# Two-block layer with a product-key expert layer: top-k and gathers interleaved, one-hot keys moved to ScalarE, weight placing split in two halves

## The chip, the cores and the metric

The kernel runs on one core of a Trainium2 chip. The metric is the device time of one execution in microseconds (us); the median of three runs is compared. A core has five engines that each run their own instruction stream in program order: PE (TensorE, matmuls), DVE (VectorE), ACT (ScalarE), POOL (GpSimd) and SP (SyncE, which here only starts transfers). They meet through semaphores.

## The reference, cut to what matters

256 tokens of width 2048 pass through two transformer blocks in fp32. The change touches only the expert layer near the end of the second block:

```python
def peer(xn, w_pq, sub_k1, sub_k2, expert_u, expert_v):
    q = (xn @ w_pq).reshape(B, S, 8, 2, 128)          # 8 heads, 2 halves
    s1, s2 = scores of q[..., 0, :] and q[..., 1, :]   # 128 sub-keys each
    v1, i1 = lax.top_k(s1, 16); v2, i2 = lax.top_k(s2, 16)
    cand = (v1[..., :, None] + v2[..., None, :]).reshape(B, S, 8, 256)
    vs, ci = lax.top_k(cand, 16)
    e1 = take(i1, ci // 16); e2 = take(i2, ci % 16)
    eidx = e1 * 128 + e2                               # one of 16384 experts
    gates = softmax(vs)
    act = gelu(einsum('tkd,td->tk', expert_u[eidx], x))     # k: 8 heads x 16 = 128
    return einsum('tk,tkd->td', act * gates, expert_v[eidx])
```

(Two lines are put in words.) So each token picks 128 experts; for each it needs a row of `expert_u` (2048 numbers, 8 KB) and a row of `expert_v`.

## The kernel before

Tokens lie on the 128 partitions, in two halves of 128 tokens (tt = 0, 1). The expert layer runs in these stages, with the span's microseconds of the profiled execution:

- **Top-k (1524 to 1666).** While PE ends the query projection (`project1`), `topk` (L1587) works through the 8 heads one after the other, two generators taking every second head. DVE finds the top 16 of each key half (MAX, MAX_INDEX, MATCH_REPLACE), POOL adds the 16 x 16 candidates (L1600), DVE finds their top 16, POOL splits each winner's position into row and column with seven small operations (L1605 to L1611), DVE compares these with 0..15 (four one-hot compares of 256, L1617), POOL multiplies by the key numbers (four products, L1618), DVE sums (four reduces, L1623) and POOL forms the expert index (six operations, L1625 to L1627). `slots_` then makes e1T, e2T (the two key numbers of each slot, transposed).
- **u rows (1666 to 2312).** `u_rows` gathers for each of the 256 slots (128 for each half of the tokens) one row per token: an indirect DMA of 128 x 8 KB = 1 MB that POOL issues (L1661), into one of 10 buffers in the first half and 4 in the second. DVE multiplies and sums it with the token (L1695, "sum" from here on), which frees the buffer. The first 10 gathers are issued in one block as soon as head 0 has its index; sums start when all heads have theirs. After the 128th sum PE turns the other tokens into PSUM (`turn`, L1657), and `weights` makes the slot weights w of the half that is done.
- **Weights into the table.** The left half of `expert_v`'s columns is not gathered. `spots(tt)` builds the dense table G (16384 experts x 256 tokens, in 8 slabs G0 to G7 of 16 key numbers e1 each): for a group of 8 tokens it makes a one-hot Q of e2 and a one-hot P of e1, scales P by w, and PE multiplies them (L1752, 8 products of 128 x 128); ACT copies the result into the 8 slabs (`put`, L1729). There are 16 groups in each half. `spots(0)` runs beside the second half of the u rows: Q on ACT (Abs and Relu, L1740/41), P on DVE (L1742), scaling on ACT (L1747). `spots(1)` runs in the gap (2312 to 2393) between the last u sum and the main loop: Q and P on DVE (L1737, L1742), scaling on POOL (L1744).
- **Main loop (from 2393).** 128 chunks k of `w_vd` (512 KB each, streamed by SP through 4 buffers) x 8 matmuls (L1848) use G. Beside it `v_rows` gathers the right half of `expert_v`'s columns, 0.5 MB for each of 256 slots (L1661, 8 buffers), and DVE adds them up (L1788, L1790), two rows for each chunk. After the last row PE turns the result (L1769), and the chunks that remain follow. `L1845` lets POOL wait for each chunk's data ("beat"), which paces the gathers. The output projection comes after.

What sets the order: every stage is a Python generator in one of five lanes. `lanes.step()` runs once for each weight chunk, lane 4 (`u_rows`, `v_rows`) a second time in the main loop, and `beside()` steps lanes 2, 3 and 4 (two heads' `topk` and `u_rows`) after every second matmul of `project1`. The build therefore fixes each engine's order; what runs late holds up everything behind it on its engine.

An fp32 matmul leaves two records in the trace, so 8 matmuls are x16.

Of the kernel before, what the change touches and what calls it, by code (L numbers as in the profile page):

```python
# [15 lines left out]
T = 256  # L16
# [209 lines left out]
def program(tc, A, out, stage=99, dbg=None):  # L226
# [1304 lines left out]
    subk, qring, eg = cK(8, 2, 128), cK(4, T), cK(2, 3, 128)  # L1531
# [54 lines left out]
    def topk(first):  # L1586
# [4 lines left out]
        xf = cT(2, 16)  # L1591
        for h in range(first, 8, 2):
# [42 lines left out]
    def slots_():
# [3 lines left out]
        G.tensor_copy(gate_, eg[:, :, 2])  # L1639
# [33 lines left out]
    def u_rows():  # L1673
        seat = [n % 10 if n < 128 else n % 4 for n in range(256)]
        m, busy = 0, {}
        for n in range(256):
            tt, s = divmod(n, 128)
            if n == 0:
                turn(0)
                while not all(flags.get(("idx", h)) for h in range(8)):  # L1680
                    while m < 10 and flags.get(("idx", m // 16)):
                        gather(row[seat[m]], A["w_u"], m)
                        busy[seat[m]] = m
                        m += 1
                    yield
# [217 lines left out]
```

## Time and profile before

| | before |
|---|---|
| median of 3 runs | 3009.86 us (3007.61 to 3015.71) |
| profiled execution, its own time | 3011.99 us |
| its span on the core | 3010.2 us |
| PE busy | 2274.8 us (76%) |
| DVE busy | 2035.2 us (68%) |
| ACT busy | 985.2 us (33%) |
| POOL busy | 936.6 us (31%) |
| first u sum starts | 1665.79 us |
| last u sum ends | 2311.55 us |
| main loop starts | 2393.40 us |
| last of the v rows turned, remaining chunks start | 2858.05 us |

An engine's share is an average over stages with different limits: PE is at work nearly all of the time in the first 1500 us and nearly idle during the u rows. What a stage is worth is read from the stage itself: which wait ends last in it, and whether the DMA engines are full.

### The profile page before, as it was taken

To read this page: it belongs to the slowest core of one execution; us is meant where nothing else is said; L and a number is where in the kernel's file an instruction comes from. 1 tells how busy PE (TensorE), PEld (TensorE's weight loads), DVE (VectorE), ACT (ScalarE), POOL (GpSimd) and SP (SyncE) were. 2 spreads that over 40 slices of the span, in tenths; PEclk is the share of its full clock that TensorE was granted. 3 is DMA by queue.
4 is the path that set the end of the run, shared out by engine and by line. 5 is a ranking of instruction groups with operands and counts; after the bars stand their busy time and mean duration, and the time that the engine had idled before them with its cause. 6 is when DMAs were issued, how large, how long until landed. Compare 5 with 4: busy or idle time off the path is not lost.

```text
span 3010.2 us, 38442 instructions
## 1 busy us (share of the span) xinstructions
PE 2274.8 (76%) x14379; PEld 2059.6 (68%) x14379; DVE 2035.2 (68%) x2663; ACT 985.2 (33%) x1952; POOL 936.6 (31%) x1281
## 2 busy tenths in 40 slices
PE   8999999999999999999978000022111699999899
PEld 8877898888889999998967000022110687877689
DVE  5555566555556565656447999989897966666646
ACT  4355554444444454444411000055530200000043
POOL 3202225111110000330145433333334755555420
PEclk9999999999999999999989555555555899999999
DMA  6443455555655555544564899999998599999945
GB/s 221 153 127 120 132 162 186 189 189 187 196 189 189 183 182 183 163 133 128 196 239 125 334 422 422 422 383 385 385 397 342 176 409 410 409 409 409 365 151 165
DMA packets 174668, 765.04 MB, mean 254 GB/s; under 512 B 19584, under 2 KB 22048, under 8 KB 141200
## 3 DMA queue, kind: packets, MB, share of 16 engines
q1 hardware_dynamic: 99216, 353.83, 35.6%
q0 software_dynamic: 75264, 408.75, 34.0%
q8 instruction: 113, 1.85, 0.3%
q14 instruction: 75, 0.61, 0.1%
HBM read 757.77 MB, written 4.21 MB: 253 GB/s over the span
## 4 chain that ended last, share of the span: by engine, by line
PE 51%; DMA 21%; issue 9%; DVE 9%; POOL 8%; ACT 1%; SPq 0%; POOLq 0%; DVEq 0%; ACTq 0%
DMA rows<-w_vs,idx 13%; PE acc L411 11%; DMA rows<-w_u,idx 7%; PE acc L386 6%; PE acc L388 6%; PE acc L387 6%; PE acc L412 6%; POOL rows L1661 5%; DVE rows L1695 3%; PE acc L485 3%; PE acc L483 3%; PE acc L484 3%; PE acc L1848 1%; PE acc L456 1%; DVE sacc L1790 1%
## 5 line engine op out<-in xcount | busy, mean ns | idle before, releaser
L350 DVE TENSOR_TENSOR wlo<-raw,whi 128x1024 fp32r<-128x1024 f32 (+1 forms) x501 | 613.8, 1233 | 418.4 <-ACT whi L349 411.5
L349 ACT CAST whi<-raw 128x1024 fp32r<-128x1024 f32 (+1 forms) x501 | 519.9, 1042 | 385.2 <-PE acc L387 131.2
L1695 DVE SCALAR_TENSOR_TENSOR rows<-rows,yt 128x2048 f32<-128x2048 f32 x256 | 579.1, 2286 | 48.4 <-DMA rows<-w_u,idx 45.7
L1848 PE MATMUL acc<-G,raw 128*128 128x256 f32 x2048 | 459.8, 385 | 25.7 <-DMA raw<-w_vd 23.7
L1848 PEld LDWEIGHTS acc<-G,raw 128*128 128x128 f32 x2048 | 390.5, 193 | 94.4 <-DMA raw<-w_vd 39.3
L1790 DVE SCALAR_TENSOR_TENSOR sacc<-rows,sm,sacc 128x1024 f32<-128x1024 f32 x254 | 327.3, 1289 | 155.1 <-DMA rows<-w_vs,idx 152.8
L1661 POOL DMA_INDIRECT rows<-w_u,idx x256 | 251.1, 981 | 385.2 <-DVE rows L1695 260.3
L1661 POOL DMA_INDIRECT rows<-w_vs,idx x256 | 255.2, 997 | 201.6 <-DVE sacc L1790 153.3
L1752 PE MATMUL sp<-P,Q 128*128 128x128 f32 x512 | 104.7, 388 | 220.6 <-ACT P L1747 187.2
L1752 PEld LDWEIGHTS sp<-P,Q 128*128 128x128 f32 x512 | 96.9, 292 | 228.4 <-ACT P L1747 191.6
L411 PE MATMUL acc<-xl,whi 128*128 128x512 f32 x704 | 248.3, 392 | 0.0
L411 PE MATMUL acc<-xh,whi 128*128 128x512 f32 x704 | 248.2, 391 | 0.0
L1657 PE MATMUL yt<-keep,xg 128*128 128x128 f32 x32 | 5.4, 342 | 304.1 <-DVE rows L1695 303.5
L564 POOL TENSOR_TENSOR acc_sq<-acc_sq,sq 128x256 f32<-128x256 f32 x63 | 56.9, 903 | 504.5 <-ACT sq L563 502.7
L1657 PEld LDWEIGHTS yt<-keep,xg 128*128 128x128 f32 x32 | 5.0, 182 | 304.7 <-DVE rows L1695 303.9
L485 PE MATMUL acc<-ring,wlo 128*128 128x256 f32 x704 | 199.3, 283 | 0.1
L483 PE MATMUL acc<-ring,whi 128*128 128x256 f32 x704 | 199.3, 283 | 0.1
L484 PE MATMUL acc<-ring,whi 128*128 128x256 f32 x704 | 199.2, 283 | 0.0
L412 PE MATMUL acc<-xh,wlo 128*128 128x256 f32 x704 | 197.2, 280 | 0.0
L412 PE MATMUL acc<-xl,wlo 128*128 128x256 f32 x704 | 197.1, 280 | 0.0
L1191 POOL TENSOR_TENSOR hT<-cF 128x256 f32<-128x256 f32 x44 | 70.9, 1611 | 372.6 <-ACT whi L349 342.7
L386 PE MATMUL acc<-xl,whi 128*128 128x256 f32 x520 | 153.2, 295 | 0.0
(476 smaller groups left out, 5343.7 us busy)
## 6 DMA issues: line engine op xcount, KB each, us to landing
raw<-w_gu SPq DMA_DIRECT2D x176, 512.0 KB, 4.2
raw<-w_vd SPq DMA_DIRECT2D x128, 512.0 KB, 6.8
raw<-w_down SPq DMA_DIRECT2D x88, 512.0 KB, 4.4
raw<-w_out SPq DMA_DIRECT2D x32, 512.0 KB, 3.6
raw<-w_pq SPq DMA_DIRECT2D x32, 512.0 KB, 3.6
raw<-w_pg SPq DMA_DIRECT2D x32, 512.0 KB, 4.0
raw<-w_b SPq DMA_DIRECT2D x24, 512.0 KB, 3.6
raw<-w_lat SPq DMA_DIRECT2D x18, 512.0 KB, 3.6
```

Of the source, the lines that this page charges most:

```text
L349: S.copy(hi[j][:, a:b], raw[j][:, a:b])
L350: V.tensor_sub(lo[j][:, a:b], raw[j][:, a:b], hi[j][:, a:b].bitcast(F32))
L386: PE.matmul(ps, wh, xh, start=start, stop=False, **k)
L411: PE.matmul(ps, wh, xh.both(k), start=k == 0, stop=False, skip_group_check=True)
L412: PE.matmul(ps[:, :T], wl, xh[:, k], start=False, stop=k == kb - 1, skip_group_check=True)
L483: PE.matmul(o, wh, ah, start=(k == 0 and j % 2 == 0), stop=False, skip_group_check=True)
L484: PE.matmul(o, wh, al, start=False, stop=False, skip_group_check=True)
L485: PE.matmul(o, wl, ah, start=False, stop=(k == nk - 1), skip_group_check=True)
L1661: G.indirect_dma_start(dst, None, src, bass.IndirectOffsetOnAxis(ap=idx[:, tt, s:s + 1], axis=0))
L1695: V.scalar_tensor_tensor(r, r, 1.0, accT, op0=OP.mult, op1=OP.mult, accum_out=wv[:, tt, s:s + 1])
L1790: V.scalar_tensor_tensor(sacc, r, w, sacc, op0=OP.mult, op1=OP.add)
L1848: PE.matmul(o, w, gs_[k // 16][:, k % 16], start=(k == 0 and j % 2 == 0), stop=k == 127, skip_group_check=True)
```

## The change

It has five parts.

1. **Top-k.** The four compares become one of 1024, ahead of the four POOL products; the four reduces become one; POOL's six index operations become three over both halves of the tokens. The exponential is emitted one step later, and there is one step more between products and reduce. The key numbers now lie in `ek`, and `slots_` copies them (4 POOL copies) before the transposes.
2. **u rows.** One gather per step instead of ten in a block, and the sums start when 4 of the 8 heads have their indices.
3. **`spots(0)`.** P is made on ACT like Q: 16 more ACT operations for each group, no DVE operation.
4. **`spots(1)`.** Two halves of 64 key numbers. Half 0 (G0 to G3) is placed before the main loop, with P of 64 columns and 4 copies for each group. Half 1 (G4 to G7) is placed inside the loop's first 62 chunks: Q and scaling on ACT, narrow P on DVE, one group every 4 chunks.
5. **`v_rows`.** The first 8 gathers are issued two per step, and never more than two per step after that.

The diff, cut to its core:

```diff
@@ topk
+            io = iota[:, 0:16][:, None, :].to_broadcast([128, 64, 16])
+            yield
+            sel = oh.rearrange("p t s a b -> p (t s a) b")
+            V.tensor_tensor(sel, flat(c1)[:, :, None].to_broadcast([128, 64, 16]), io, op=OP.is_equal)
+            for tt, s in both:
+                G.tensor_mul(oh[:, tt, s], oh[:, tt, s], iif[:, tt, s][:, None, :].to_broadcast([128, 16, 16]))
             for tt in range(2):
-                S.activation(eg[:, tt, 2, hs], vs[:, tt], AF.Exp, bias=gs[:, tt, 0:1], accum_out=gs[:, tt, 1:2])
-            io = iota[:, 0:16][:, None, :].to_broadcast([128, 16, 16])
-            yield
-            for tt, s in both:
-                V.tensor_tensor(oh[:, tt, s], c1[:, tt, s][:, :, None].to_broadcast([128, 16, 16]), io, op=OP.is_equal)
-                G.tensor_mul(oh[:, tt, s], oh[:, tt, s], iif[:, tt, s][:, None, :].to_broadcast([128, 16, 16]))
-            yield
-            yield
+                S.activation(eg[:, tt, hs], vs[:, tt], AF.Exp, bias=gs[:, tt, 0:1], accum_out=gs[:, tt, 1:2])
+            yield
+            yield
+            yield
+            V.tensor_reduce(flat(ek[:, h]), sel, axis=AX.X, op=OP.add)
             V.reciprocal(gs[:, :, 2], gs[:, :, 1])
-            for tt, s in both:
-                V.tensor_reduce(eg[:, tt, s, hs], oh[:, tt, s], axis=AX.X, op=OP.add)
...
@@ u_rows
+        def more(most):
+            while most and ask[0] < 256 and seat[ask[0]] not in busy and flags.get(("idx", ask[0] % 128 // 16)):
+                m = ask[0]
+                gather(row[seat[m]], A["w_u"], m)
+                busy[seat[m]] = m
+                ask[0] += 1
+                most -= 1
...
+        while heads() < 4:
+            more(1)
+            yield
         for n in range(256):
             tt, s = divmod(n, 128)
-            if n == 0:
-                turn(0)
-                while not all(flags.get(("idx", h)) for h in range(8)):
-                    while m < 10 and flags.get(("idx", m // 16)):
-                        gather(row[seat[m]], A["w_u"], m)
...
+            for _ in range(2 if heads() < 8 else 0):
+                more(1)
                 yield
+            more(2)
+            while n >= ask[0]:
+                yield
+                more(1)
...
@@ spots
+        if not tt:
+            for n in range(16):
...
+                lit(Q, i, t0)
                 for k in range(8):
-                    S.activation(Q[:, k], iota, AF.Abs, bias=gs_["n"][:, t0 + k:t0 + k + 1])
-                    S.activation(Q[:, k], Q[:, k], AF.Relu, scale=-1.0, bias=one)
-            V.tensor_tensor(P, io, e1T[:, ts][:, :, None].to_broadcast(wide), op=OP.is_equal)
...
+                    S.activation(P[:, k], iota, AF.Abs, bias=gs_["m"][:, t0 + k:t0 + k + 1])
+                    S.activation(P[:, k], P[:, k], AF.Relu, scale=-1.0, bias=one)
...
+        else:
+            for half in range(2):
+                lo, p = half * 64, None
+                for n in range(16):
...
+                    if half:
+                        lit(Q, i, t0)
+                    else:
+                        V.tensor_tensor(Q, io, e2T[:, ts][:, :, None].to_broadcast(wide), op=OP.is_equal)
+                    Pn = P[:, :, 0:64]
+                    V.tensor_tensor(Pn, iota[:, lo:lo + 64][:, None, :].to_broadcast(narrow),
+                                    e1T[:, ts][:, :, None].to_broadcast(narrow), op=OP.is_equal)
+                    if half:
+                        for k in range(8):
+                            S.activation(P[:, k, 0:64], P[:, k, 0:64], AF.Identity, scale=wT[:, t0 + k:t0 + k + 1])
+                        for _ in range(2):
+                            yield
+                    else:
+                        G.tensor_mul(Pn, Pn, wT[:, ts][:, :, None].to_broadcast(narrow))
...
+                    for k in range(8):
+                        PE.matmul(p[:, at + k * 64:at + k * 64 + 64], Q[:, k], P[:, k, 0:64], start=True, stop=True)
...
+                    if half and n % 2:
+                        put(range(4, 8), t0 - 8, p, 16)
+                    elif not half:
+                        put(range(4), t0, p[:, 0:512], 8)
+                    yield
+                flags[("g", 1, half)] = True
@@ v_rows
-            while m < 256 and m % 8 not in busy:
...
+            for _ in range(4 if n == 0 else 1):
+                for _ in range(2):
+                    if m < 256 and m % 8 not in busy:
...
+                if n == 0:
+                    yield
@@ main loop
-    until(("g", 1))
+    until(("g", 1, 0))
...
+        if k == 62:
+            until(("g", 1, 1))
```

`lit` is the pair of ACT loops that made Q before, as a function.

**DVE, around the fifth head (head 4).** Before, one head from the index search to the next head's first MAX (L1617 compares, L1621 reciprocal, L1623 reduces):

```order
L1583 MAX_INDEX cT<-cT 128x8 x2
L1617 TENSOR_TENSOR cT<-cT,keep 128x256 x4
L1621 RECIPROCAL cT<-cT 128x2
L1623 TENSOR_REDUCE cK<-cT 128x16 x4
L1572 MAX cT<-sc 128x8 x4
```

After, the end of head 4 (L1703 is the u sum, L1616 the merged compare, L1624 the merged reduce):

```order
L1580 MAX cT<-cT 128x8 x2
L1703 SCALAR_TENSOR_TENSOR rows_15108,sm<-rows_15108,yt 128x2048
L1583 MAX_INDEX cT<-cT 128x8 x2
L1616 TENSOR_TENSOR cT<-cT,keep 128x1024
L1703 SCALAR_TENSOR_TENSOR rows_15108,sm<-rows_15108,yt 128x2048
L1624 TENSOR_REDUCE cK<-cT 128x64
L1625 RECIPROCAL cT<-cT 128x2
L1703 SCALAR_TENSOR_TENSOR rows_15109,sm<-rows_15109,yt 128x2048 x2
L1703 SCALAR_TENSOR_TENSOR rows_15110,sm<-rows_15110,yt 128x2048
L1572 MAX cT<-sc 128x8 x4
```

Between the reduce of head 3 and that of head 7 there now stand 25 sums on DVE (6, 7, 7 and 5 for the four heads); before there was none. One of them stands between every compare and its reduce.

**POOL, behind the first head's index.** Before (L1661 is the gather, L1632 the gate, L1598 to L1600 the next head's candidates):

```order
L1627 CAST idx<-cT 128x16
L1661 DMA rows_15106<-w_u,idx 128x2048 x2
L1661 DMA rows_15107<-w_u,idx 128x2048 x2
L1661 DMA rows_15108<-w_u,idx 128x2048 x2
L1661 DMA rows_15109<-w_u,idx 128x2048 x2
L1661 DMA rows_15110<-w_u,idx 128x2048 x2
L1632 TENSOR_SCALAR cK<-cK,cT 128x16 x2
L1598 CAST cT<-cT 128x64
L1600 TENSOR_TENSOR cT<-cT 128x256 x2
```

After (L1663 is the gather, L1601 the candidates):

```order
L1628 CAST idx<-cT 128x2x16
L1663 DMA rows_15106<-w_u,idx 128x2048
L1633 TENSOR_SCALAR cK<-cK,cT 128x16 x2
L1599 CAST cT<-cT 128x64
L1601 TENSOR_TENSOR cT<-cT 128x256 x2
L1663 DMA rows_15106<-w_u,idx 128x2048
L1663 DMA rows_15107<-w_u,idx 128x2048 x2
L1663 DMA rows_15108<-w_u,idx 128x2048 x2
L1606 CAST cT<-cT 128x32
```

The ten gathers no longer stand ahead of the candidates of the next head in one block; 10 stand ahead of head 4's index, and 34 ahead of head 7's.

**PE, from the second half's groups on.** Before (L1752 a group's products, L1848 the loop's matmuls, L1769 the turning of the v sums, L386 the output projection; x128 is 16 chunks):

```order
L1752 MATMUL sp<-P,Q 128x128 x128
L1848 MATMUL acc<-G_16381,raw 128x256 x128
...
L1848 MATMUL acc<-G_16388,raw 128x256 x56
L1769 MATMUL tok<-keep,rows_15106 128x128 x8
L1848 MATMUL acc<-G_16388,raw 128x256 x72
L386 MATMUL acc<-pl,whi 128x256
```

After (L1794 the groups, L1900 the loop, L1815 the turning):

```order
L1794 MATMUL sp<-P,Q 128x64 x128
L1900 MATMUL acc<-G_16313,raw 128x256 x8
L1794 MATMUL tok<-P,Q 128x64 x8
L1900 MATMUL acc<-G_16313,raw 128x256 x32
L1794 MATMUL tok<-P,Q 128x64 x8
...
L1900 MATMUL acc<-G_16320,raw 128x256 x64
L1815 MATMUL tok<-keep,rows_15106 128x128 x8
L1900 MATMUL acc<-G_16320,raw 128x256 x64
L386 MATMUL acc<-pl,whi 128x256
```

All 128 products of half 0 stand ahead of the loop; the 16 groups of half 1 stand inside it, the first after one chunk, then one every four. Behind the last turning stand 8 chunks instead of 9. On DVE 12 v sums stand ahead of the loop instead of 16.

## Rows read from the trace of the kernel before

**Rows 1.** Windows: stretch, length, each engine's busy time (instructions), PEclk, DMA share, GB/s
```profile
1524.00:1666.00 142.00, 97.24 (x460) 83.94 (x459) 100.83 (x457) 18.69 (x78) 76.51 (x180) 0.87 0.50 171
...
2312.00:2393.00 81.00, 45.23 (x257) 41.66 (x257) 69.03 (x52) 23.25 (x130) 67.01 (x44) 0.73 0.47 151
2393.00:2845.00 452.00, 427.41 (x1911) 362.94 (x1912) 299.70 (x235) 2.07 (x6) 243.24 (x350) 0.98 1.03 408
```

**Rows 2.** Timeline, DVE, top-k: start, duration, line, operation, count [idle before <-releaser]
```profile
1560.62 1.00 DVE L1572 MAX8 cT<-cT 128x8 f32<-128x256 f32 x2 [12.88 <-POOL cT L1600]
...
1602.49 0.86 DVE L1572 MAX8 cT<-sc 128x8 f32<-128x128 f32 x4
...
1608.16 1.00 DVE L1572 MAX8 cT<-cT 128x8 f32<-128x256 f32 x2 [0.91 <-POOL cT L1600]
...
1613.58 0.42 DVE L1617 TENSOR_TENSOR cT<-cT,keep 128x256 f32<-128x256 f32 x1 [1.39 <-POOL cT L1608]
1614.52 2.15 DVE L1617 TENSOR_TENSOR cT<-cT,keep 128x256 f32<-128x256 f32 x3 [0.52 <-POOL cT L1610]
...
1665.79 2.28 DVE L1695 SCALAR_TENSOR_TENSOR rows<-rows,yt 128x2048 f32<-128x2048 f32 x1
...
1667.99 2.28 DVE L1695 SCALAR_TENSOR_TENSOR rows<-rows,yt 128x2048 f32<-128x2048 f32 x1
```

**Rows 3.** Timeline, POOL, first and last of ten gathers behind head 0's index
```profile
1546.87 1.08 POOL L1661 DMA_INDIRECT rows<-w_u,idx  x1 [0.18 <-issue]
...
1558.21 0.94 POOL L1661 DMA_INDIRECT rows<-w_u,idx  x1 [0.30 <-issue]
```

**Rows 4.** Groups by line, top-k stretch: count | busy, mean ns | idle before
```profile
L1618 POOL TENSOR_TENSOR cT<-cT 128x256 f32<-128x256 f32 x32 | 26.4, 853 | 0.0
```

**Rows 5.** Timeline, DVE, second half of the u rows
```profile
1973.65 2.29 DVE L1695 SCALAR_TENSOR_TENSOR rows<-rows,yt 128x2048 f32<-128x2048 f32 x1 [2.41 <-PE yt L1657]
...
1998.29 2.29 DVE L1695 SCALAR_TENSOR_TENSOR rows<-rows,yt 128x2048 f32<-128x2048 f32 x1 [0.19 <-DMA rows<-w_u,idx]
...
2000.78 2.29 DVE L1695 SCALAR_TENSOR_TENSOR rows<-rows,yt 128x2048 f32<-128x2048 f32 x1 [0.19 <-DMA rows<-w_u,idx]
```

**Rows 6.** Groups by line, second half of the u rows: the one-hot P
```profile
L1742 DVE TENSOR_TENSOR P<-keep,sq 128x1024 f32<-128x1024 f32 x16 | 19.5, 1220 | 0.0
```

**Rows 7.** Timeline, ACT, first group beside the u rows: pairs, scaling, copies
```profile
1973.92 0.40 ACT L1740 ACTIVATE Q<-keep,ne 128x128 f32<-128x128 f32 x1
...
1979.75 2.43 ACT L1747 ACTIVATE P<-P,acc_sq 128x128 f32<-128x128 f32 x8
1983.84 1.45 ACT L1729 COPY G<-sp 128x128 f32<-128x128 f32 x8 [1.66 <-PE sp L1752]
```

**Rows 8.** Timeline, DVE, gap before the main loop: first group, two later ones
```profile
2311.55 1.22 DVE L1737 TENSOR_TENSOR Q<-keep,sq 128x1024 f32<-128x1024 f32 x1
...
2349.51 2.01 DVE L1737 TENSOR_TENSOR Q<-keep,sq 128x1024 f32<-128x1024 f32 x1
...
2353.77 2.01 DVE L1737 TENSOR_TENSOR Q<-keep,sq 128x1024 f32<-128x1024 f32 x1
```

**Rows 9.** Timeline, POOL, same gap: first scaling, slowest of the first gathers
```profile
2314.31 1.90 POOL L1744 TENSOR_TENSOR P<-P,acc_sq 128x1024 f32<-128x1024 f32 x1 [1.23 <-DVE P L1742]
...
2325.39 1.91 POOL L1661 DMA_INDIRECT rows<-w_vs,idx  x1 [0.30 <-DVE sacc L1790]
```

**Rows 10.** Timeline, PE: a group, the loop's start, and its end
```profile
2363.27 2.05 PE L1752 MATMUL sp<-P,Q 128*128 128x128 f32 x16 [0.62 <-POOL P L1744]
...
2393.40 133.10 PE L1848 MATMUL acc<-G,raw 128*128 128x256 f32 x608 [1.54 <-ACT G L1729]
2526.95 3.72 PE L1848 MATMUL acc<-G,raw 128*128 128x256 f32 x16 [0.44 <-DMA raw<-w_vd]
...
2856.29 1.97 PE L1769 MATMUL tok<-keep,rows 128*128 128x128 f32 x8 [10.75 <-ACT rows L1797]
2858.05 32.56 PE L1848 MATMUL acc<-G,raw 128*128 128x256 f32 x144
```

More of the change, by code (lines that the diff above doesn't have):

```diff
@@ L1591, in topk @@
         xf = cT(2, 16)
+        flat = lambda v: v.rearrange("p t s n -> p (t s n)")
         for h in range(first, 8, 2):
@@ L1638, in slots_ @@
             yield
[L1639 removed]
+        G.tensor_copy(gate_, eg)
         for tt in range(2):
@@ L1674, in u_rows @@
         seat = [n % 10 if n < 128 else n % 4 for n in range(256)]
-        m, busy = 0, {}
+        done, busy, ask = [0], {}, [0]
+        def more(most):
[5 more added lines that the diff above has]
+                most -= 1
+        heads = lambda: sum(bool(flags.get(("idx", h))) for h in range(8))
+        turn(0)
+        while heads() < 4:
+            more(1)
+            yield
         for n in range(256):
             tt, s = divmod(n, 128)
-            if n == 0:
-                turn(0)
-                while not all(flags.get(("idx", h)) for h in range(8)):
-                    while m < 10 and flags.get(("idx", m // 16)):
-                        gather(row[seat[m]], A["w_u"], m)
-                        busy[seat[m]] = m
-                        m += 1
-                    yield
-            while True:
-                while m < 256 and seat[m] not in busy and flags.get(("idx", m % 128 // 16)):
-                    gather(row[seat[m]], A["w_u"], m)
-                    busy[seat[m]] = m
-                    m += 1
-                if n < m:
-                    break
+            for _ in range(2 if heads() < 8 else 0):
+                more(1)
                 yield
+            more(2)
+            while n >= ask[0]:
+                yield
+                more(1)
             r = row[seat[n]]
@@ L1723, in spots, with lit @@
+        wide, narrow = [128, 8, 128], [128, 8, 64]
         io = iota[:, None, :].to_broadcast(wide)
[L1725 to L1745 removed]
+        def lit(Q, i, t0):
+            for k in range(8):
+                S.activation(Q[:, k], iota, AF.Abs, bias=gs_["n"][:, t0 + k:t0 + k + 1])
+                S.activation(Q[:, k], Q[:, k], AF.Relu, scale=-1.0, bias=one)
@@ new lines, in put @@
+        def put(groups, t0, p, nt):
+            pv = p.rearrange("p (t i) -> p i t", t=nt)
+            for a, g in enumerate(groups):
+                S.copy(gs_[g][:, :, t0:t0 + nt], pv[:, 16 * a:16 * a + 16])
+        if not tt:
+            for n in range(16):
+                i = n % 2
+                Q, P = gs_["Q", i], gs_["P", i]
+                t0 = n * 8
+                ts = slice(t0, t0 + 8)
+                lit(Q, i, t0)
+                for k in range(8):
+                    S.activation(P[:, k], iota, AF.Abs, bias=gs_["m"][:, t0 + k:t0 + k + 1])
+                    S.activation(P[:, k], P[:, k], AF.Relu, scale=-1.0, bias=one)
@@ L1746, in spots @@
                 for k in range(8):
                     S.activation(P[:, k], P[:, k], AF.Identity, scale=wT[:, t0 + k:t0 + k + 1])
-            if not tt:
                 yield
-            p = pair("sp")
-            for k in range(8):
-                PE.matmul(p[:, k * 128:k * 128 + 128], Q[:, k], P[:, k], start=True, stop=True)
-            for _ in range(0 if tt else 4):
-                yield
-            put(n, p)
-            yield
+                p = pair("sp")
+                for k in range(8):
+                    PE.matmul(p[:, k * 128:k * 128 + 128], Q[:, k], P[:, k], start=True, stop=True)
```

54 lines of the change are left out of this document (26 added, 28 removed).

## The prediction, made before the changed kernel was run

> **What bounds the kernel now.** I read the stretches of the expert layer first, engine by engine and with the DMA's share [rows 1]. In the top-k stretch the DMA engines are half idle (0.50, 171 GB/s) and DVE is busy 100.83 of 142 us. In the gap between the last u sum and the main loop they are again at 0.47. In the main loop they are full (1.03, 408 GB/s), with PE at 427.41 of 452 us just below. So the layer is a train of transfers with two holes, and the change works on the holes. Then the timelines. In top-k, DVE goes through the heads one by one and waits for POOL in each [rows 2]; the ten first gathers stand on POOL in one block from 1546.87 to 1559.15 [rows 3], and DVE waits 12.88 us behind it [rows 2]. The first u sum starts at 1665.79 [rows 2], with the ten buffers long full. In the second half of the u rows, sums come 2.49 us apart (1998.29 to 2000.78) and wait for the transfer [rows 5]: the DMA's pace for 1 MB. In the gap DVE repeats a cycle of 4.26 us (2349.51 to 2353.77) [rows 8]. In the loop PE first runs 38 chunks without a break, 133.10 us or 3.50 each, then waits for `w_vd` [rows 10].
>
> **A. Top-k and the start of the u rows.** Between head 3's and head 7's reduce 25 sums now stand on DVE. Each that is done there frees a buffer, so a gather runs in the hole of the DMA; at 2.49 us a row [rows 5] this takes 25 x 2.49 = 62 us from the stage behind. Against it, head 7 is ready later. From 1602.49, where head 4 begins, to 1665.79 four heads take 63.3 us, 15.8 each [rows 2]. Of this DVE waits 0.91 + 1.39 + 0.52 = 2.8 for POOL [rows 2], and its four compares (0.42 + 2.15 us) become one of 1024 numbers, for which I take the 1.22 of the one-hot P of that size [rows 6]. That leaves 15.8 - 2.8 - 1.3 = 11.7 of work; the merged reduce I leave at its price. Four heads are 47 us, and 25 sums at 2.20 from start to start (1665.79 to 1667.99) [rows 2] are 55. Waits stay: the four products of 0.85 [rows 4] are 3.4 us on POOL between compare and reduce, and the reduce now needs all four, where the sum put between them covers 2.2; gathers stand on POOL as well. I take 2 us for each head, 8. Sum 110 instead of 63.3, or +47. In the first four heads the block of 12.3 us is spread, but compare and reduce wait for more; I credit 4. Net 62 - 47 + 4 = 19, say **-20**. Bounds: with every wait hidden and 8 credited, -31; with waits of 5 us for each head, -5. A loss is not excluded (rival 1).
>
> What is late behind it: nothing new. After head 7, 103 sums of 2.20 (227 us) face some 94 rows of 2.49 (234 us), so the DMA still sets the pace.
>
> **B. P off DVE in the second half of the u rows.** The 128 sums from 1973.65 to 2311.55 [rows 5, 8] take 337.9 us, 2.64 each, where the transfer alone needs 2.49. P is there 16 times, 19.5 us in all [rows 6]; with four buffers, each holds back the next gathers. Without it 128 x 2.49 = 318.7, at most -19; I take **-17**. The cover is ACT: a group now has two sets of eight Abs/Relu pairs, 1979.75 - 1973.92 = 5.83 each, the scaling 2.43, the wait for PE 1.66 and the copies 1.45 [rows 7]; 17.2 us, 16 groups 275, under 319. If a group took 20, ACT would end after the u rows and hold up the slot weights, which stand behind it. Bounds -4 and -19.
>
> **C. The gap.** From 2311.55 [rows 8] to the loop's start at 2393.40 [rows 10] are 81.9 us: 2.8 until POOL's first scaling (2314.31 [rows 9]), a ragged start, and cycles of 4.26 made of Q (2.01), P (1.22 alone) and a v sum. Now P and its scaling on POOL have half the columns: P costs 0.61 less. Q alone is 1.22 (2311.55) and beside POOL's scaling of 1.90 it is 2.01 [rows 8, 9]; with half the scaling I take half of that excess, 0.4. Cycle 4.26 - 0.6 - 0.4 = 3.3. The first five groups have no v sum, and POOL sets them: five scalings of 0.95 and eight gathers of 1.23 (ten span 12.3 [rows 3]), 14.6. Then 11 x 3.3 = 36.3, and 2.5 for the last PE group and copies. 2.8 + 14.6 + 36.3 + 2.5 = 56.2: **-25**. Bounds: with no excess left, 2.9 a cycle, -30; with all of it, 3.65, and the eight gathers as slow as the slowest (1.91 [rows 9], 0.8 more each), -15.
>
> That Q takes 2.01 instead of 1.22 only while POOL scales is what the rows show [rows 8, 9]. [...]
>
> **D. The loop.** Half 1 adds 16 PE groups to the first 62 chunks. A full group takes 2.05 at best [rows 10]; with half the columns an estimate between 1.03 and 2.05, I take 1.5: 24 us. The first group stands after one chunk and needs Q and scaled P from ACT, 5.83 + 2.43 = 8.3 [rows 7] after the last copy of half 0, against 3.5 of PE work: a stop of 5. The first 62 chunks take 62 x 3.5 + 24 + 5 = 246. Before, PE ran 38 chunks at 3.50 and then at the transfer's pace: 452 us from 2393 to 2845 for 119 chunks [rows 1, 10], so (452 - 133) / 81 = 3.94. After the 62 the 38 free chunks come again: 246 + 133 + 20 x 3.94 = 458 for 120 chunks, 6 more than now. By the transfers: 12 v sums instead of 16 stand ahead of the loop, four rows of 0.5 MB or 5 us more. These two are alternatives, not a sum. Behind the last turning 8 chunks follow instead of 9 (32.56 / 9 = 3.6 less [rows 10]). 6 - 3.6 plus small stops of about 2: **+4**. Bounds -2 (groups at 1.03, no stop) and +14 (2.05 each, more stops).
>
> The new wait: PE's matmuls of four chunks are queued behind each group, which waits for ACT's scaling, which waits for DVE's P, which stands behind about eight v sums. P stands two chunks ahead of its products, 7.9 us.
>
> **The sum.** -20 - 17 - 25 + 4 = -58. The profiled execution took 3011.99, 2.1 above the median of the runs; 3011.99 - 58 - 2.1 = **2952** on the median's footing.
>
> **Rivals.**
>
> 1. Top-k gains nothing. The chain compare, products, reduce, index runs to and fro between DVE and POOL; gathers on POOL and sums on DVE may lengthen each step. For it: each head has three waits today [rows 2], and the gathers do stand between. Against: sums fill these waits. It decides where a head takes 11 us more than I sum up, 20 / 4 = 5 more each and the credit of 4 gone. A = 0: 2952 + 20 = 2972.
>
> 2. Half groups cost as much as full ones. 16 x 2.05 = 33 us [rows 10] instead of 24, and each group stops PE for about 1 us more: +9 and +16 on PE's side, 25. Then PE, not the transfers, bounds the first 62 chunks: 2952 + 25 = 2977 if all of it stays. For it: a group of 8 products is short, and the loop's PE has only 452 - 427 = 25 us to spare [rows 1]. Against: PE regains 0.44 us with each chunk that the transfers bound. [...]
>
> 3. Slower: the groups stop PE every time. If ACT's Q and scaling lay open in front of each of the 16, 16 x 8.3 = 132 us [rows 7], of which I have counted 5: 2952 + 127 = 3079. It decides where DVE lies more than 7.9 us behind PE: then scaled P comes too late at every group. It turns the sign where a stop is above 62 / 16 = 3.9. For it: at the loop's end PE waits 10.75 us for the last v sums [rows 10], more than 7.9. Against: a stop brings PE back by its own length, and while PE stands the DMA goes on with v rows, so the lag is not paid anew each time.
>
> 4. The second half's u rows don't get faster: the 2.64 come from ACT's and PE's work beside them and not from P. B = 0: 2969. For it: the sums wait for the transfer also between two P. Against: sums right behind each other after P, and 19.5 us of P against 19 of loss.
>
> **How the numbers follow.** Forecast (2932 to 2965) 0.60, rival 1 0.14, rival 2 0.12, rival 4 0.07, rival 3 0.05, and 0.02 for small gains that cancel. The range reaches down to 2930, near the sum of the good bounds (-31 - 19 - 30 - 2 = -82, 2928), and up to 2984, over rivals 1, 2 and 4 with some of each other's loss; rival 3 stays out. A measurement can tell 0.3% from no change, 9 us. All cases but rival 3 and the last are more than that below 3010: faster 0.92, same 0.03, slower 0.05.
>
> **What would show it.** A right: 25 sums before head 7's reduce, that reduce at 1700 to 1715, the first half's last sum near 1950 (now 1970). B: sums 2.49 apart on the whole of the second half, an ACT group of about 17. C: 54 to 60 us from the last u sum to the loop's first matmul. D: a stop of about 5 us in front of the first group in the loop, little in front of the others, DMA still full there, and 8 chunks behind the turning. Wrong: head 7 beyond 1730; a u pace of 2.6; a gap above 66; PE waiting for ACT's scaling at each group.

## The result and the profile after

The changed kernel takes 2965.32 us, median of 4 runs (2960.12 to 2975.14), against 3011.07 (3007.61 to 3015.71): a ratio of 0.9848, 95% interval 0.9829 to 0.9866, or 45.7 us less. The profiled execution took 2963.08 us (span 2961.3), 48.9 less than the one of before. Of these 48.9, 4.6 lie ahead of the expert layer: the first top-k instruction starts at 1519.16 instead of 1523.79, in code that the change doesn't touch; in the profiled executions shown below that moment wanders between 1519 and 1536. So every stage is measured from that instruction.

Before, DVE timeline (start, duration, line, operation, count, idle before and what ended it):

```profile
1523.79 0.30 DVE L1572 MAX8 cT<-sc 128x8 f32<-128x128 f32 x1 [14.89 <-ACT sc L1555]
```

| stage | before | after | difference | predicted |
|---|---|---|---|---|
| A: first top-k instruction to the end of the first half's sums | 446.2 | 424.6 | -21.6 | -20 |
| between the halves | 3.6 | 3.8 | +0.2 | 0 |
| B: the 128 sums of the second half | 337.9 | 322.5 | -15.4 | -17 |
| C: last u sum to the loop's first matmul | 81.8 | 63.0 | -18.8 | -25 |
| D: loop to the last turning, and the chunks behind it | 497.2 | 508.3 | +11.1 | +4 |
| sum | | | -44.5 | -58 |

The stages' ends are read from the DVE and PE timelines of the two profiles. After, DVE in top-k and at the start of the second half; these answer [rows 2, 5]:

```profile
1519.16 0.29 DVE L1572 MAX8 cT<-sc 128x8 f32<-128x128 f32 x1 [14.89 <-ACT sc L1555]
...
1592.87 1.22 DVE L1624 TENSOR_REDUCE cK<-cT 128x64 f32<-128x1024 f32 x1 [2.90 <-POOL cT L1618]
1594.08 2.27 DVE L1703 SCALAR_TENSOR_TENSOR rows<-rows,yt 128x2048 f32<-128x2048 f32 x1
...
1616.00 1.23 DVE L1616 TENSOR_TENSOR cT<-cT,keep 128x1024 f32<-128x1024 f32 x1 [2.46 <-POOL cT L1611]
1617.14 2.28 DVE L1703 SCALAR_TENSOR_TENSOR rows<-rows,yt 128x2048 f32<-128x2048 f32 x1
...
1620.13 1.22 DVE L1624 TENSOR_REDUCE cK<-cT 128x64 f32<-128x1024 f32 x1 [0.70 <-POOL cT L1618]
...
1700.81 1.22 DVE L1624 TENSOR_REDUCE cK<-cT 128x64 f32<-128x1024 f32 x1 [1.52 <-POOL cT L1618]
...
1947.62 2.29 DVE L1703 SCALAR_TENSOR_TENSOR rows<-rows,yt 128x2048 f32<-128x2048 f32 x1 [3.77 <-PE yt L1659]
...
1974.61 2.29 DVE L1703 SCALAR_TENSOR_TENSOR rows<-rows,yt 128x2048 f32<-128x2048 f32 x1 [0.20 <-DMA rows<-w_u,idx]
...
1977.10 2.29 DVE L1703 SCALAR_TENSOR_TENSOR rows<-rows,yt 128x2048 f32<-128x2048 f32 x1 [0.19 <-DMA rows<-w_u,idx]
...
2270.10 1.22 DVE L1779 TENSOR_TENSOR Q<-keep,sq 128x1024 f32<-128x1024 f32 x1
```

The first sum starts at 1594.08, 71.7 us earlier than before. The wait in front of a reduce, 2.90 us without a sum before it, is 0.70 with one. Between 1974.61 and 1977.10 the pace of the transfers is as before, and no P stands between. Now the windows of after (PE, PEld, DVE, ACT, POOL busy; granted clock; DMA share; GB/s), which answer [rows 1]:

```profile
1594.00:1702.00 108.00, 43.48 (x185) 36.85 (x183) 98.76 (x256) 8.41 (x34) 55.14 (x101) 0.70 0.77 287
...
1947.00:2270.00 323.00, 61.01 (x260) 56.16 (x258) 293.32 (x255) 238.41 (x769) 116.53 (x124) 0.55 0.99 405
2270.00:2333.00 63.00, 56.41 (x257) 55.17 (x257) 50.03 (x50) 13.04 (x67) 42.38 (x40) 0.50 0.51 162
2333.00:2580.00 247.00, 243.77 (x1229) 216.59 (x1230) 170.53 (x142) 128.68 (x413) 131.38 (x187) 0.98 1.01 397
2580.00:2796.00 216.00, 207.62 (x947) 178.48 (x947) 142.88 (x113) 1.91 (x6) 117.09 (x169) 0.99 1.02 406
```

The third line holds the surprise: in the gap PE is busy 56.41 of 63 us, at a granted clock of 0.50. PE's timeline of after, from the gap to the loop's end, answers [rows 10]:

```profile
2282.44 3.68 PE L1794 MATMUL sp<-P,Q 128*128 128x64 f32 x16 [0.77 <-POOL P L1789]
...
2290.97 41.22 PE L1794 MATMUL sp<-P,Q 128*128 128x64 f32 x192 [0.58 <-POOL P L1789]
2333.05 6.01 PE L1900 MATMUL acc<-G,raw 128*128 128x256 f32 x16 [0.86 <-ACT G L1745]
2339.10 2.11 PE L1794 MATMUL tok<-P,Q 128*128 128x64 f32 x16
...
2341.05 14.03 PE L1900 MATMUL acc<-G,raw 128*128 128x256 f32 x64
2354.92 1.89 PE L1794 MATMUL tok<-P,Q 128*128 128x64 f32 x16
...
2505.60 7.17 PE L1900 MATMUL acc<-G,raw 128*128 128x256 f32 x32 [1.43 <-DMA raw<-w_vd]
...
2809.84 1.97 PE L1815 MATMUL tok<-keep,rows 128*128 128x128 f32 x8 [11.38 <-ACT rows L1847]
2811.60 29.77 PE L1900 MATMUL acc<-G,raw 128*128 128x256 f32 x128
```

Twelve groups in a row take 41.22 us, 3.43 each: from 2290.97 on PE runs without a break and sets the gap's pace. Ahead of that it waits for POOL in front of each group (0.77, 0.58). In the loop a group costs 1.73 us (from its start at 2354.92 to the next chunk at 2356.65), and no wait stands in front of it.

### The profile page after: what moved, and what is told of

Its sections match the earlier page's. It is cut to its first block, busy times and chain, and to the rows that moved or that the text cites. A ratio compares the mean times of both kernels' runs of the same rounds, so it can differ in the third digit from the quotient of the medians.

```text
span 2961.3 us, 39499 instructions
## 1 busy us (share of the span) xinstructions
PE 2311.8 (78%) x14635; PEld 2106.1 (71%) x14635; DVE 1999.7 (68%) x2615; ACT 1191.2 (40%) x2560; POOL 900.9 (30%) x1262
## 4 chain that ended last, share of the span: by engine, by line
PE 59%; DMA 12%; DVE 10%; issue 9%; POOL 8%; ACT 1%; another core or an unknown queue 0%; SPq 0%; POOLq 0%; DVEq 0%; ACTq 0%
PE acc L411 11%; PE acc L1900 7%; PE acc L386 6%; PE acc L388 6%; PE acc L387 6%; DMA rows<-w_vs,idx 6%; PE acc L412 6%; POOL rows L1663 5%; DMA rows<-w_u,idx 5%; DVE rows L1703 5%; PE acc L485 3%; PE acc L483 3%; PE acc L484 3%; PE sp L1794 1%; DMA raw<-w_vd 1%
## 5 line engine op out<-in xcount | busy, mean ns | idle before, releaser
L1703 DVE SCALAR_TENSOR_TENSOR rows<-rows,yt 128x2048 f32<-128x2048 f32 x256 | 580.3, 2285 | 42.9 <-DMA rows<-w_u,idx 38.6
L1900 PE MATMUL acc<-G,raw 128*128 128x256 f32 x2048 | 457.3, 385 | 12.4 <-DMA raw<-w_vd 11.1
L1900 PEld LDWEIGHTS acc<-G,raw 128*128 128x128 f32 x2048 | 391.8, 193 | 71.7 <-DMA raw<-w_vd 17.0
L1663 POOL DMA_INDIRECT rows<-w_u,idx x256 | 244.2, 954 | 380.0 <-DVE rows L1703 274.8
L1663 POOL DMA_INDIRECT rows<-w_vs,idx x256 | 248.8, 972 | 149.6 <-DVE sacc L1840 81.7
L1762 PE MATMUL sp<-P,Q 128*128 128x128 f32 x256 | 60.2, 430 | 213.9 <-ACT P L1758 213.9
L1762 PEld LDWEIGHTS sp<-P,Q 128*128 128x128 f32 x256 | 55.8, 330 | 218.6 <-ACT P L1758 218.6
L386 PE MATMUL acc<-xh,whi 128*128 128x256 f32 x520 | 150.6, 290 | 3.2 <-ACT whi L349 1.8
```

The source lines that it names most:

```text
L386: PE.matmul(ps, wh, xh, start=start, stop=False, **k)
L1663: G.indirect_dma_start(dst, None, src, bass.IndirectOffsetOnAxis(ap=idx[:, tt, s:s + 1], axis=0))
L1703: V.scalar_tensor_tensor(r, r, 1.0, accT, op0=OP.mult, op1=OP.mult, accum_out=wv[:, tt, s:s + 1])
L1900: PE.matmul(o, w, gs_[k // 16][:, k % 16], start=(k == 0 and j % 2 == 0), stop=k == 127, skip_group_check=True)
```

## The experiments

All experiments start from the changed kernel. What was read from each profile, with the same stages (the last column is the time from the last u sum to the end of the loop's matmuls):

| kernel | median, us | ratio to before (95%) | A | B | gap | gap + loop to its end |
|---|---|---|---|---|---|---|
| before | 3011.07 | 1 | 446.2 | 337.9 | 81.8 | 579.0 |
| after | 2965.32 | 0.9848 (0.9829 to 0.9866) | 424.6 | 322.5 | 63.0 | 571.3 |
| u1_no_A | 2987.44 | 0.9902 (0.9879 to 0.9925) | 445.6 | 324.3 | 63.0 | 567.0 |
| a1_sums_after8 | 2994.91 | 0.9943 (0.9922 to 0.9964) | 447.0 | 322.8 | 63.2 | 570.7 |
| a2_sums_after1 | 2947.51 | 0.9793 (0.9768 to 0.9818) | 407.1 | 322.6 | 63.2 | 567.6 |
| u2_no_B | 2978.90 | 0.9869 (0.9841 to 0.9897) | 424.2 | 340.7 | 63.0 | 568.6 |
| u3_no_C | 2974.68 | 0.9866 (0.9843 to 0.9889) | 424.2 | 325.5 | 77.3 | 575.9 |
| w1_wide | 2962.72 | 0.9832 (0.9803 to 0.9862) | 425.1 | 322.5 | 56.8 | 565.6 |
| v1_old | 2972.04 | 0.9880 (0.9856 to 0.9904) | 424.8 | 322.6 | 67.6 | 574.8 |
| d1_few_groups | 2963.39 (one run) | | 424.4 | 322.2 | 62.9 | 566.4 |
| b1_both | 2943.94 | 0.9766 (0.9741 to 0.9791) | 407.1 | 325.3 | 57.2 | 567.3 |

Where two kernels have the same gap and loop (after, u1, a1, a2, u2), the last column still differs by up to 4.3 us (567.0 to 571.3, mean 569.0), and where P is on ACT, B differs by up to 3.3 (322.2 to 325.5). Differences below that are not read.

### Part A: what of it is the interleaving

u1_no_A puts `topk`, `slots_` and `u_rows` of before back.

> Top-k and u_rows as before, all else as after (P on ACT, split spots, paced v gathers). Theory: part A is worth what its stage shows, 21.6 us (last u sum of the first half 26.2 us earlier, of which 4.6 us lie ahead of the first top-k instruction); so about 2965 + 22 = 2987 us, the 128 sums of the second half still in 322 us, the gap 63 us, loop to the last turning 478 us. Rival: A only moved waiting time, the gain belongs to B and C; then 2965 to 2970 us.

It took 2987.44 us, with A back at 445.6: the rival falls. a1_sums_after8 keeps the merged operations and the spread gathers, and only starts the sums late:

```diff
-        while heads() < 4:
+        while heads() < 8:
```

> As after, but the u sums start when all 8 heads have their indices instead of 4: merged top-k operations and spread first gathers stay, no sum stands among the heads. Theory (A's whole gain is the rows that flow while heads 4 to 7 are worked on; merging alone is worth nothing): head 7's reduce ends about 143 us after the first top-k instruction (before 142.1, after 182.9), the first half ends at 446 (after 424.6), 2965 + 22 = 2987 us. Rival (merging itself shortens the heads): head 7's reduce at 132 or less, first half's end at 436 or less, 2976 us or less.

A is 447.0, so the merged operations and the spread gathers alone are worth nothing. DVE in a1_sums_after8, one head:

```profile
1633.68 1.00 DVE L1572 MAX8 cT<-cT 128x8 f32<-128x256 f32 x2 [0.91 <-POOL cT L1601]
...
1639.79 1.23 DVE L1616 TENSOR_TENSOR cT<-cT,keep 128x1024 f32<-128x1024 f32 x1 [2.09 <-POOL cT L1611]
...
1643.91 1.22 DVE L1624 TENSOR_REDUCE cK<-cT 128x64 f32<-128x1024 f32 x1 [2.89 <-POOL cT L1618]
...
1650.79 1.00 DVE L1572 MAX8 cT<-cT 128x8 f32<-128x256 f32 x2 [0.91 <-POOL cT L1601]
```

A head takes 17.1 us (1633.68 to 1650.79), against 15.8 before, and waits 5.9 of it: the merged reduce waits 2.89 for all four products, where the four separate reduces of before followed them one by one. Merging lengthens a head; its waits are what the sums fill. The median, 2994.91, is 8 us above what was expected. In the profiled execution (3001.77) the stages differ by the 22.4 of A alone; its first top-k instruction stands at 1536.1, 16.9 us later than in after, in code that no experiment touches.

If waits are what the sums fill, sums in heads 1 to 3 must gain as well:

```diff
-        while heads() < 4:
+        while heads() < 1:
```

> As after, but the u sums start when the first head has its indices: 40 sums ahead of head 7's reduce instead of 25. Theory (sums fill DVE's waits in heads 1 to 3 and keep the transfers going): 15 more rows taken from the stage behind, 37 us, against 15 x 2.2 = 33 us of DVE less the 15 to 20 us of waits that they fill; first half's end 15 to 20 us earlier, at 405 to 410 after the first top-k instruction, 2948 us. Rival (the added sums wait for their rows and hold up top-k): first half's end at 420 to 430, 2962 to 2970 us.

A falls to 407.1, 17.5 less, and the kernel to 2947.51 us, ratio 0.9793. DVE and the window from head 1 to head 7 in a2_sums_after1:

```profile
1557.25 2.29 DVE L1703 SCALAR_TENSOR_TENSOR rows<-rows,yt 128x2048 f32<-128x2048 f32 x1 [3.01 <-DMA rows<-w_u,idx]
...
1729.29 1.22 DVE L1624 TENSOR_REDUCE cK<-cT 128x64 f32<-128x1024 f32 x1 [1.52 <-POOL cT L1618]
```

```profile
1555.00:1731.00 176.00, 79.66 (x321) 66.97 (x319) 159.65 (x404) 14.63 (x60) 98.46 (x175) 0.73 0.88 346
```

Only the first sum waits for its row (3.01). DVE is busy 159.65 of 176 us: little is left there for more sums to fill.

### Part B

u2_no_B puts P of the first half's groups back on DVE:

```diff
-                for k in range(8):
-                    S.activation(P[:, k], iota, AF.Abs, bias=gs_["m"][:, t0 + k:t0 + k + 1])
-                    S.activation(P[:, k], P[:, k], AF.Relu, scale=-1.0, bias=one)
+                V.tensor_tensor(P, io, e1T[:, ts][:, :, None].to_broadcast(wide), op=OP.is_equal)
```

> P of the first half's groups back on DVE, Q on ACT, all else as after. Theory (P on DVE costs the u rows time): the 128 sums of the second half take 337 to 338 us instead of 322.5, 2965 + 15 = 2980 us. Rival 4 of the prediction (P on DVE costs nothing, the 2.64 came from what ACT and PE do beside): they stay at 322 to 325 us, 2965 to 2968 us.

The 128 sums take 340.7 us, 18.2 more than after; rival 4 falls. DVE in u2_no_B (without the accumulator reads between):

```profile
1979.38 2.29 DVE L1703 SCALAR_TENSOR_TENSOR rows<-rows,yt 128x2048 f32<-128x2048 f32 x1 [0.19 <-DMA rows<-w_u,idx]
...
1981.59 1.22 DVE L1754 TENSOR_TENSOR P<-keep,sq 128x1024 f32<-128x1024 f32 x1
1982.73 2.28 DVE L1703 SCALAR_TENSOR_TENSOR rows<-rows,yt 128x2048 f32<-128x2048 f32 x1
...
1990.05 2.29 DVE L1703 SCALAR_TENSOR_TENSOR rows<-rows,yt 128x2048 f32<-128x2048 f32 x1 [0.61 <-DMA rows<-w_u,idx]
```

After each P sums stand right behind each other (DVE is late), and then one waits again, 0.61 and not the usual 0.19. I read this as the buffer that was freed late behind P coming back late.

### Part C: the gap

u3_no_C places the second half's groups whole in the gap, with products of 128 columns and POOL's full scaling, as before; nothing of it stands in the loop.

```diff
-            for half in range(2):
...
+            for n in range(16):
...
+                V.tensor_tensor(Q, io, e2T[:, ts][:, :, None].to_broadcast(wide), op=OP.is_equal)
+                V.tensor_tensor(P, io, e1T[:, ts][:, :, None].to_broadcast(wide), op=OP.is_equal)
+                G.tensor_mul(P, P, wT[:, ts][:, :, None].to_broadcast(wide))
...
+                put(range(8), t0, p, 8)
```

> The second half's groups placed whole in the gap, as before; all else as after. Theory (gap and loop add up): gap from the last u sum to the first matmul of the loop back to 82 us (now 63), loop to the last turning back to 465 us (now 478.6); balance +19 - 11 = +8, 2973 us. Rival (the split gains nothing, what the gap gives the loop takes): 2963 to 2967 us.

2974.68 us: the sign and size of the balance were as expected (gap and loop 575.9, some 7 above the 569.0 of kernels with the split), but the gap is 77.3 and not 82. The balance isn't the split's alone, since behind the last turning of u3_no_C stand 7 chunks and not 8. The missing 4.5 of the gap fit part 5, the paced gathers, which stayed in. v1_old puts the old `v_rows` back into the changed kernel:

```diff
-            for _ in range(4 if n == 0 else 1):
-                for _ in range(2):
-                    if m < 256 and m % 8 not in busy:
+            while m < 256 and m % 8 not in busy:
...
```

> As after, but v_rows asks for its first 8 rows in one block and for any number in a step later, as before. Theory (the paced gathers shorten the gap, by letting POOL's scalings through): gap 66 to 70 us instead of 63.0, 2969 us. Rival (pacing is worth nothing in the gap, PE's groups at the lower granted clock set it): gap 63, 2965 us.

Gap 67.6, 4.6 more. POOL in v1_old shows why: behind the first scaling come all eight gathers, and the second scaling starts at 2284.76, 11.7 us after the first, with the groups behind it.

```profile
2273.07 1.04 POOL L1789 TENSOR_TENSOR P<-P,acc_sq 128x512 f32<-128x512 f32 x1 [0.91 <-ACT acc_sq L1672]
2274.26 0.98 POOL L1663 DMA_INDIRECT rows<-w_vs,idx  x1
...
2283.36 1.38 POOL L1663 DMA_INDIRECT rows<-w_vs,idx  x1 [0.30 <-issue]
2284.76 1.05 POOL L1789 TENSOR_TENSOR P<-P,acc_sq 128x512 f32<-128x512 f32 x1
```

The prediction counted POOL's scalings and gathers as one sum and had no term for the order among them. In the last column v1_old is 5.8 above the mean of 569.0, but there 10 chunks stand behind the last turning instead of 8, so only the gap is read.

What held the gap at 63.0, where I had 56.2? PE's groups, by the timeline of after. w1_wide lets the half-0 groups multiply all 128 columns of P (the other 64 left over and not copied), with the same number of instructions:

```diff
-                        PE.matmul(p[:, at + k * 64:at + k * 64 + 64], Q[:, k], P[:, k, 0:64], start=True, stop=True)
+                        PE.matmul(p[:, k * 128:k * 128 + 128], Q[:, k], P[:, k], start=True, stop=True)
...
-                        put(range(4), t0, p[:, 0:512], 8)
+                        put(range(4), t0, p, 8)
```

> The half-0 groups in the gap multiply all 128 columns of P (64 of them left over from earlier groups and not copied), same number of instructions; copies and everything else as after. Theory (a group's price is the load of its stationary operand, 128 columns either way): a group stays at 3.4 to 3.7 us at the lower granted clock and the gap at 61 to 65 us, 2965 us; if the granted clock rises with the wider products, groups fall to 2.05 and the gap to 54 to 58 us, 2958 us. Rival (price by columns of the moving operand): groups of 6.9 to 7.3 us, gap about 115 us, 3015 us.

Twice the columns, and the gap is shorter: 56.8 us. PE and the gap's window in w1_wide:

```profile
2278.11 6.72 PE L1797 MATMUL sp<-P,Q 128*128 128x128 f32 x32 [2.11 <-POOL P L1789]
2285.73 2.05 PE L1797 MATMUL sp<-P,Q 128*128 128x128 f32 x16 [0.89 <-POOL P L1789]
2290.98 5.50 PE L1797 MATMUL sp<-P,Q 128*128 128x128 f32 x32 [3.20 <-POOL P L1789]
2297.61 2.05 PE L1797 MATMUL sp<-P,Q 128*128 128x128 f32 x16 [1.13 <-POOL P L1789]
...
2318.77 2.05 PE L1797 MATMUL sp<-P,Q 128*128 128x128 f32 x16 [0.96 <-POOL P L1789]
```

```profile
2273.90:2330.70 56.80, 37.32 (x257) 34.02 (x257) 48.20 (x49) 13.05 (x67) 48.67 (x37) 0.88 0.54 169
```

With the wide products the granted clock of the gap is 0.88 instead of 0.50. The third group already takes 2.05 us; the next two take 5.50 together, and from 2297.61 on every group takes 2.05 and waits about 0.96 for POOL's scaled P. From 2285.70 to 2330.70 the granted clock is 0.96 on average; in before, groups of 2.05 us stand at 1.00 (2380.31). The cycle is then 3.02 us, and DVE has no wait in it: Q, P and a v sum start 1.22, 0.61 and 1.19 us apart (2303.43 to 2306.45). So the 6.2 us by which the gap of after is longer than this one are PE at a granted clock of 0.50. Why the clock stays down with the narrow products isn't shown; only that it does, in all seven profiles that have them in the gap (after, u1, a1, a2, u2, v1, d1): the granted clock of the gap is 0.50 in each.

### Part D: the loop

d1_few_groups multiplies only the first two of the 16 groups in the loop; the copies of the other groups take the result of those two, and 14 x 16 records of PE are left out.

```diff
-                    if half == 0 or n % 2 == 0:
+                    if half == 0 or n == 0:
                         p = pair("tok" if half else "sp")
...
-                    for k in range(8):
+                    for k in range(8 if half == 0 or n < 2 else 0):
```

> As after, but of the 16 groups inside the loop only the first two are multiplied on PE; the copies of the other 14 take the result of those two, so part of the weights in G4 to G7 is wrong and 14 x 16 records of PE are left out. Theory (PE with the groups bounds the first 62 chunks): these take 14 x 1.73 = 24 us less on PE, down to the transfers' pace; loop to the last turning 476.8 - 6 to -13, 464 to 471 us. Rival (the transfers bound the loop all along, the longer loop is the four more v rows): 475 to 477 us.

24 us of PE work gone shorten the loop to the last turning to 472.5: 4.3 less than in after (476.8), 2.9 less than the mean of the five kernels with the same loop (473.6 to 477.0, mean 475.4). That is between the theories, nearer to the rival's 475, and hardly more than the spread. PE in d1_few_groups:

```profile
2362.59 121.08 PE L1900 MATMUL acc<-G,raw 128*128 128x256 f32 x560
...
2500.03 33.92 PE L1900 MATMUL acc<-G,raw 128*128 128x256 f32 x144 [5.43 <-DMA raw<-w_vd]
```

After 35 chunks without a break it waits for `w_vd`: what PE saves it waits for. The loop is bound by the transfers; the groups cost at most 3 to 4 us on top, which this one run doesn't tell from the spread. The rest of the longer loop I put down to bytes, by an estimate that no run tests alone. In the gap of before the DMA moved 151 GB/s for 81.8 us [rows 1], 12.4 MB; in after 162 GB/s for 63.0 us, 10.2 MB. The 2.2 MB that the shorter gap no longer moves take 5.3 us at 408 GB/s in the loop.

### Both gains together

b1_both is a2_sums_after1 and w1_wide in one kernel.

> After with the two edits that gained most, put together: sums from the first head's index on, and half-0 groups with products of all 128 columns in the gap. Theory (the two lie in different stages and add): first half's end at 407 after the first top-k instruction, gap 57, 2965 - 17.5 - 5.7 = 2942 us. Rival (the shorter gap only hands its transfers to the loop, so the wide products are worth nothing in the end): gap 57 but the loop longer by as much, 2948 us as with the early sums alone.

2943.94 us, ratio 0.9766 (0.9741 to 0.9791): faster than before, and than after (0.9848). But against a2_sums_after1 (0.9793) the intervals overlap, and gap and loop together take 567.3 against 567.6. Of the 6 us that the wide products take from the gap, w1_wide kept 3.4 against the mean of the others (565.6 against 569.0) and b1_both 1.7. Whether they are worth 0 or 3 us isn't settled; the rival, that the loop takes most of it back, has the better of it.

## Why the prediction came out as it did

The forecast was 2952 in a range of 2930 to 2984; measured 2965.32, in the range, faster as said, 46 us instead of 58. By the stages A came out 1.6 us better and B 1.6 worse than forecast; C is 6 short and D 7 worse.

- **A held in its parts.** Heads 4 to 7 with 25 sums take 107.9 us (1594.08 to 1702.02), predicted 110; the first four heads gain 3.8, predicted 4; from head 7 to the end of the half 241.7 instead of 304.2, 62.5 less, predicted 62. a1 and a2 show the mechanism from both sides. Rival 1 falls.
- **B held:** -15.4 for -17; u2_no_B gives it back, so rival 4 falls. The cover on ACT was there: it is busy 238 of 323 us.
- **C: two steps failed.** "POOL sets them" held for the first groups, but not its price of 14.6; and PE, which I took for hidden behind a cycle of 3.3 us, was the bound of that cycle. The forecast's sum against two gaps, from POOL's rows:

| term, us | forecast | after | w1_wide |
|---|---|---|---|
| until POOL's first scaling | 2.8 | 2.4 | 2.4 |
| five scalings and eight gathers on POOL | 14.6 | 18.4 | 18.0 |
| eleven cycles | 36.3 | 37.5 | 33.4 |
| the last PE group and copies | 2.5 | 4.6 | 3.0 |
| gap | 56.2 | 63.0 | 56.8 |

POOL in the gap of after, first scaling to fifth and the last; it has no wait for another engine from 2272.54 to 2290.91:

```profile
2272.54 1.68 POOL L1789 TENSOR_TENSOR P<-P,acc_sq 128x512 f32<-128x512 f32 x1 [0.91 <-ACT acc_sq L1672]
...
2281.33 1.05 POOL L1789 TENSOR_TENSOR P<-P,acc_sq 128x512 f32<-128x512 f32 x1
2282.54 1.79 POOL L1663 DMA_INDIRECT rows<-w_vs,idx  x1 [0.16 <-issue]
2284.64 0.94 POOL L1663 DMA_INDIRECT rows<-w_vs,idx  x1 [0.30 <-issue]
...
2289.86 1.05 POOL L1789 TENSOR_TENSOR P<-P,acc_sq 128x512 f32<-128x512 f32 x1
...
2327.37 1.04 POOL L1789 TENSOR_TENSOR P<-P,acc_sq 128x512 f32<-128x512 f32 x1 [1.24 <-DVE P L1781]
```

Of the 6.8 us that the gap is longer than forecast, 3.8 are POOL's: scalings of 1.05 to 1.68 instead of 0.95, and gathers of which some took 1.79. PE at a granted clock of 0.50, at 3.43 a group, makes the cycle 3.41; with PE at 2.05 a group (w1_wide, granted clock 0.96 from 2285.70 on) the cycles take 4.1 us less and the end 1.7 less. That w1_wide's 56.8 meets my 56.2 is luck: its first groups are 3.4 longer and its eleven cycles 2.9 shorter than I had them. A row of before that I didn't weigh had PE's price: it took 3.65 for some groups, inside a cycle of 4.26. Shortening the cycle to 3.3 put that price above it. PE in the gap of before:

```profile
2376.05 3.65 PE L1752 MATMUL sp<-P,Q 128*128 128x128 f32 x16 [1.19 <-POOL P L1744]
2380.31 2.05 PE L1752 MATMUL sp<-P,Q 128*128 128x128 f32 x16 [0.61 <-POOL P L1744]
```

My rival 2, "half groups cost as much as full ones", had the right price in the wrong stage. A group that waits on both sides takes 3.68 us with 64 columns (after, 2282.44, granted clock 0.50) and 3.65 with 128 (before, 2376.05, granted clock 0.54). From one record's start to the next inside a group, the traces have 112 ns at a granted clock of 1.00 and 213 ns at 0.50, with 64 columns (after) and with 128 (before). The loads of the stationary operand are recorded as 128x128 with either width, and the 16 loads of a group take 3.48 us at 0.50 with either (after, 2282.44; before, 2316.26). That these loads set the price fits the rows; no run changes them alone.
- **C, contention:** Q beside half the scaling is 1.58 to 1.77 in after and 1.30 in w1_wide; I took 2.01 - 0.4 = 1.6. But the prediction read the rows of before wrongly: it set Q against the whole scaling of 1.90, and when Q starts most of a us of it is over. POOL and DVE in the gap of before, then DVE in that of after (beside the scaling from 2281.33, shown above):

```profile
2348.54 1.90 POOL L1744 TENSOR_TENSOR P<-P,acc_sq 128x1024 f32<-128x1024 f32 x1 [0.43 <-DVE P L1742]
...
2349.51 2.01 DVE L1737 TENSOR_TENSOR Q<-keep,sq 128x1024 f32<-128x1024 f32 x1
...
2281.71 1.77 DVE L1779 TENSOR_TENSOR Q<-keep,sq 128x1024 f32<-128x1024 f32 x1 [1.90 <-PE sp L1794]
```

Where Q starts during a scaling, it is longer than its 1.22 by what is left of the scaling, less about 0.13: by 0.79 with 0.93 left (before), by 0.55 with 0.68 and 0.36 with 0.49 left (after), by 0.08 with 0.21 left (w1_wide). The gathers' issue is held up in the same way, by Q: 1.79 instead of 0.98 where Q had 0.93 left, which the prediction had only in its bound (1.91 each).
- **D: the step that failed is "These two are alternatives, not a sum".** A sum fits better: rows that aren't moved in the gap (5.3 us by the bytes), one chunk more ahead of the turning (3.7, of which the shorter tail gives back 2.8), and PE's groups (at most 3 to 4 by d1_few_groups) make up to 10; measured 11.1 in after, 8.8 by the mean of the five kernels with its gap and loop (569.0 - 63.0 against 497.2). How much of it each of the three is stays open: no run takes out the bytes alone, and d1_few_groups is near the spread. The stop of 5 us in front of the first group wasn't there: the first chunk took 6.01 us, at a granted clock of 0.61, instead of 3.5, and PE's group starts at 2339.10, 0.4 us after ACT's first of eight scalings (2338.72 to 2340.72), not after the last. In w1_wide, where the first chunk took 3.72, the first group did wait for ACT, 2.33 us; chunk and wait together are 6.0 us in both, against 8.5 in the forecast. Rival 3 falls: in after no group waits for ACT, though DVE lies as far behind PE at the end (11.38) as before (10.75).

C and D belong together, since from the last u sum on the same rows and chunks have to move. The gap gained 18.8 and the loop gave back 11.1; 7.7 is left. The idle time of the DMA in the gap fell by 12: 81.8 x (1 - 0.47) = 43 before, 63.0 x (1 - 0.51) = 31 after. That the gain goes by this idle time is an account after the fact, and two runs don't follow it: by it v1_old (share 0.59) would gain 16 and u3_no_C (0.41) lose 2, and they gained 4.2 and 3.1, with 10 and 7 chunks behind the last turning.

## What to carry to other kernels

Where the transfers bound what follows, a hole in front of it is worth less than its length: here a gap 18.8 us shorter left a gain of 7.7. How much less, the runs don't settle. Work that waits for another engine at each step is the place for independent work that frees buffers; merging small operations there gained nothing by itself (447.0 us against 446.2), and the one big operation waits for all its inputs (2.89 us a head in a1_sums_after8). Halving a matmul's moving columns, 128 to 64, didn't lower its price here, with the stationary operand 128 wide (112 ns a record with either at a granted clock of 1.00), so an engine that had room in a stage may become its bound when everything else in it is halved. Before a collision of two engines is priced, look at how much of the first instruction is left when the second starts (0.93 of 1.90 us in before).

## What the runs showed of the hardware

- Products of 64 columns against a stationary operand of 128 cost as much as products of 128 columns: 112 ns from record to record at a granted clock of 1.00 and 213 ns at 0.50 (groups of after against those of before).
- With the 64-column groups nearly back to back (PE busy 56.41 of 63 us) the granted clock of the gap was 0.50; with 128-column groups that left PE idle a third of the time (37.32 of 56.8) it was 0.88. Doing twice the multiplications made the stage 6 us shorter.
- Q on DVE, started while a multiplication ran on POOL, was longer by what was left of that, less about 0.13 us (0.79 for 0.93 left in before, 0.08 for 0.21 in w1_wide). A gather's issue on POOL, started while Q ran, took 1.79 us instead of 0.98; Q started during a gather's issue took its usual 1.22 to 1.23 (after, from 2294.68 on).
